# A hybrid attention block on one core: one load queue at the start, and the first norm's row factor moved from the input tiles to the results

## The chip, the core and the metric

The kernel runs on one NeuronCore of a Trainium2 chip. The core has a matrix engine (TensorE, PE in the profile, with its weight loads as PEld), a vector engine (VectorE, DVE), an engine for functions of one operand (ScalarE, ACT), a general one (GpSimd, POOL), and SyncE (SP), which here only issues loads and stores. Matrix products go to PSUM banks; the other tiles lie in SBUF. Loads can be issued from the queues of SP, ACT and POOL. The metric is device time of one execution in microseconds; less is better.

## The reference

One layer of a hybrid block on 256 rows of width 2048, float32. The input is normalised row by row, projected by one wide matrix, mixed by three branches, and followed by a feed-forward part:

```python
def _rms_norm(x, gain):
    xf = x.astype(jnp.float32)
    y = xf * lax.rsqrt(jnp.mean(xf * xf, axis=-1, keepdims=True) + RMS_EPS)
    return (y * gain.astype(jnp.float32)).astype(x.dtype)
...
    u = _rms_norm(x, norm_mix_pre[l])
    mix = hybrid_mixer(u, w_in[l], ...)          # proj = u @ w_in; three branches, gates
    x = x + _rms_norm(mix, norm_mix_post[l])
    hdn = jnp.square(jax.nn.relu(_rms_norm(x, norm_mlp_pre[l]) @ w_mlp_up[l]))
    x = x + _rms_norm(hdn @ w_mlp_down[l], norm_mlp_post[l])
```

The branches are stick-breaking attention and forgetting attention (4 heads of 128 each) and an RWKV-7 time mixing (16 heads of 64). The norm in front of the projection multiplies row t by a factor rstd[t] and column d by a gain. So u @ w = rstd[t] * ((x * gain) @ w): the row factor can be applied to the input tiles or to the result.

## The kernel before

**Tiles and units.** Activations lie transposed, features on partitions and the 256 rows along the free axis, as 16 tiles of 128 features. The precision of float32 is made of two parts: a value is split into a rounded high part and the rest. `split` writes a tile [128, 512] with the high part in columns 0 to 255 and the rest in 256 to 511 (one copy on ACT, one subtraction on DVE). A weight block of 128 x 1024 (512 KB, eight feature tiles by 128 output columns) is loaded into a `raw` buffer and split by `wsplit` into `whi` (ACT, line 152) and `wlo` (DVE, line 153). A half unit is then eight wide products (`whi` with all 512 columns) and eight narrow ones (`wlo` with the high 256 columns); two half units make a unit, 128 output columns in one bank. `evac` empties a bank: it adds the two halves of the columns. `tok` computes value and gate tiles the other way round, with rows on partitions and 512 output columns.

**Order.** `raw`, `whi` and `wlo` have three buffers each. `wnext` keeps one half unit split ahead. Up to the end of the output projection the order on PE is the order of the code (`manual_schedule`, line 247); on the other engines and the queues a planner orders the instructions, and may put one that it holds ready ahead of one written earlier. The mixers (attention, RWKV) run as generators whose steps are placed between the products by an estimated clock (`tick`).

**The start (lines 255 to 354).** The parameters and x (`X0`, 2 MB in four pieces) are issued from ACT's queue, the weights from SP's, in whole blocks of 512 KB. `xsplit` scales x by the gain only and splits it into `xpk`, tiles without the row factor. The first three units (`qb`, weight blocks 0/1, 2/3, 4/5) run interleaved over the first eight tiles and then over the last eight, each product as soon as its tile is there. Five more units on `xpk` follow: together the stick-breaking q and k. After the fourth unit `norm()` squares X0, sums over features by a product with ones, and makes `rstd` as a tile [128, 256] that holds the factor of each row on all partitions. The eight results are multiplied by `rstd` on DVE (line 349). `normed(k)` makes the normalised tiles `upk[k]` from X0, gain and `rstd` (two DVE instructions and one ACT copy each), ten in the loop and six later beside the value tiles. All later units of the projection read `upk`.

**Results.** `shift` (line 520) empties the banks of the RWKV features and mixes each row with the one before; `vtok` (line 908) copies value tiles, `gate` (line 967) takes the tanh of half the gate logits. `rwkv_half` loads a small matrix per pair of heads into the tile `lor` (`lora_load`) and splits it (`lora_split`, line 584).

The loads at the start, as written:

```python
    nc.scalar.dma_start(out=par, in_=params)
    raws = {}
    for a, b, n in ((0, 2, 0), (2, 4, 2), (4, 8, 4), (8, 16, 1)):
        nc.scalar.dma_start(out=X0[:, a:b, :], in_=xt[:, a:b, :])
        raws[n] = wraw(n)
    side.append(lambda: nc.sync.dma_start(out=con, in_=consts[:, 128:]))
    side.append(lambda: nc.sync.dma_start(out=ident, in_=consts[:, 0:128]))
```

## Time and profile before

| | |
|---|---|
| median of 3 runs | 1515.03 us |
| lowest, highest | 1512.64, 1515.22 us |
| the profiled execution's own time | 1514.31 us |
| its span, first to last instruction | 1512.5 us |
| granted TensorE clock, mean | 0.995 |
| moved by DMA | 317.70 MB, mean 210 GB/s |

The profile is one execution. It lists each engine's busy time, the instructions by source line with their mean duration, what ended the idle time before them (the releaser), and the transfers with their time from issue to landing. A matrix product in float32 can show as more than one record. "L153" is line 153 of the kernel. A tile's name stands for all its buffers.

### The profile page before, as it was taken

Reading aid. Unit: us, or ns where it says so; the run is one execution under the profiler, and the core shown is the slowest. Engines: PE = TensorE matmul, PEld = TensorE weight load, DVE = VectorE, ACT = ScalarE, POOL = GpSimd, SP = SyncE. Lnnn points to the kernel's source line nnn. Section 1 sums busy time; section 2 is a strip of 40 time slices with the busy share of each in tenths; the row PEclk is TensorE's granted clock in tenths of the full one; section 3 lists DMA queues with packets and bytes.
Section 4 is the critical chain, followed back from the end, with each engine's and each line's share of the span. In section 5 each row is a group of like instructions: output and inputs, shape, how many; then the busy total and the mean of one; then the engine's idle time right before and its main releaser. Section 6 shows DMA issues by size and latency. Waiting matters only on the chain.

```text
span 1512.5 us, 22758 instructions
## 1 busy us (share of the span) xinstructions
PE 1479.7 (98%) x8387; PEld 1247.3 (82%) x8387; DVE 1213.7 (80%) x1675; ACT 938.4 (62%) x1408; POOL 86.1 (6%) x159
## 2 busy tenths in 40 slices
PE   7999999999999999999999999999999999999997
PEld 6888888887777887788887888888888888888885
DVE  6876677789669799567656788999899999899996
ACT  7665666654566554565444767777677676677662
POOL 0011000100001100000000000000000000000000
PEclk9999999999999999999999999999999999999999
DMA  7555445545544445445784668888879788889884
GB/s 260 184 180 171 164 168 183 172 155 194 182 146 153 166 168 180 160 147 196 252 293 159 219 207 244 245 245 264 265 234 270 243 248 253 254 249 274 251 258 150
DMA packets 107039, 317.70 MB, mean 210 GB/s; under 512 B 10672, under 2 KB 14640, under 8 KB 106544
## 3 DMA queue, kind: packets, MB, share of 16 engines
q1 hardware_dynamic: 93536, 282.76, 54.5%
q0 software_dynamic: 8064, 29.36, 10.4%
q10 hardware_dynamic: 5328, 4.13, 0.8%
q8 instruction: 66, 1.08, 0.3%
q14 instruction: 45, 0.37, 0.1%
HBM read 282.65 MB, written 4.19 MB: 190 GB/s over the span
## 4 chain that ended last, share of the span: by engine, by line
PE 49%; issue 3%; DMA 3%; DVE 1%; ACT 0%; POOL 0%; POOLq 0%; DVEq 0%; ACTq 0%
PE gps L168 13%; PE gps L214 10%; PE gps L172 7%; PE gps L198 3%; PE mps L1324 3%; PE mps L1326 3%; PE mps L1325 3%; PE gps L1326 2%; PE gps L1324 2%; PE gps L1325 2%; PE gps L176 1%; DMA raw<-in_wst_dram 1%; DMA raw<-raw 1%; DMA sp<-raw 1%; DMA sp<-in_wst_dram 1%
## 5 line engine op out<-in xcount | busy, mean ns | idle before, releaser
L153 DVE TENSOR_TENSOR wlo<-raw,whi 128x1024 fp32r<-128x1024 f32 x507 | 616.6, 1225 | 169.4 <-ACT whi L152 155.7
L152 ACT ACTIVATE whi<-raw 128x1024 fp32r<-128x1024 f32 x507 | 532.9, 1056 | 257.1 <-DMA raw<-in_wst_dram 89.8
L168 PE MATMUL gps<-pk,whi 128*128 128x512 f32 x1301 | 330.5, 393 | 0.2 <-DVE pk L1116 0.2
L214 PE MATMUL gps<-whi,pk 128*128 128x512 f32 x1144 | 289.4, 392 | 0.0
L168 PEld LDWEIGHTS gps<-pk,whi 128*128 128x128 f32 x1301 | 241.7, 189 | 47.7 <-DVE pk L1116 0.6
L214 PEld LDWEIGHTS gps<-whi,pk 128*128 128x128 f32 x1144 | 212.7, 188 | 44.2
L172 PEld LDWEIGHTS gps<-pk,wlo 128*128 128x128 f32 x1391 | 189.9, 190 | 13.4 <-DVE wlo L153 0.2
L172 PE MATMUL gps<-pk,wlo 128*128 128x256 f32 x1391 | 195.5, 283 | 0.0
L214 PE MATMUL gps<-wlo,pk 128*128 128x512 f32 x572 | 155.6, 392 | 3.1 <-DVE wlo L153 3.1
L214 PEld LDWEIGHTS gps<-wlo,pk 128*128 128x128 f32 x572 | 106.2, 188 | 26.0 <-DVE wlo L153 3.9
L1190 DVE TENSOR_TENSOR sp<-raw,sp 128x1024 fp32r<-128x1024 f32 x67 | 81.9, 1223 | 6.6 <-ACT sp L1189 6.4
L1189 ACT ACTIVATE sp<-raw 128x1024 fp32r<-128x1024 f32 x67 | 70.5, 1053 | 15.3 <-DMA raw<-in_wst_dram 5.1
L1216 ACT ACTIVATE sp<-gps 128x512 f32<-128x512 f32 x52 | 31.0, 597 | 68.6 <-PE gps L176 68.5
L198 PE MATMUL gps<-whi,pk 128*128 128x512 f32 x264 | 72.3, 396 | 1.1 <-ACT whi L152 1.1
L1324 PE MATMUL mps<-whi,fm 128*128 128x512 f32 x168 | 66.2, 394 | 0.0
L1325 PE MATMUL mps<-whi,fm 128*128 128x512 f32 x168 | 65.9, 392 | 0.0
L1326 PE MATMUL mps<-wlo,fm 128*128 128x512 f32 x168 | 65.6, 391 | 0.0
L198 PEld LDWEIGHTS gps<-whi,pk 128*128 128x128 f32 x264 | 49.6, 190 | 12.2 <-ACT whi L152 1.8
L1286 POOL DMA_DIRECT2D raw<-raw x40 | 34.9, 873 | 428.4 <-DVE raw L1283 132.7
L1326 PE MATMUL gps<-wlo,fm 128*128 128x512 f32 x126 | 49.3, 391 | 0.4 <-DVE wlo L153 0.4
L1324 PE MATMUL gps<-whi,fm 128*128 128x512 f32 x126 | 49.3, 391 | 0.0
L1283 DVE TENSOR_TENSOR raw<-raw,raw 128x1024 f32<-128x1024 f32 x40 | 48.9, 1223 | 0.4
(383 smaller groups left out, 1984.3 us busy)
## 6 DMA issues: line engine op xcount, KB each, us to landing
raw<-in_wst_dram SPq DMA_DIRECT2D x502, 512.0 KB, 4.4
raw<-raw POOLq DMA_DIRECT2D x40, 512.0 KB, 7.5
sp<-in_wst_dram SPq DMA_DIRECT2D x16, 512.0 KB, 6.0
raw<-sp POOLq DMA_DIRECT2D x8, 512.0 KB, 7.3
sp<-raw POOLq DMA_DIRECT2D x8, 512.0 KB, 7.5
x<-in_x_dram SPq DMA_DIRECT2D x8, 256.0 KB, 6.4
xs<-x SPq DMA_DIRECT2D x2, 1024.0 KB, 4.1
x<-xs SPq DMA_DIRECT2D x4, 512.0 KB, 6.0
```

Source lines behind the costliest of these rows:

```text
L152: A.activation(hi, raw, AF.Copy)
L153: V.tensor_tensor(lo, raw, hi.bitcast(F32), ALU.subtract)
L168: PE.matmul(ps, hi[:, i * 128:i * 128 + 128], pks[i], start=first and i == 0, stop=False)
L172: PE.matmul(ps[:, 0:T], lo[:, i * 128:i * 128 + 128], pks[i][:, 0:T], start=False, stop=False)
L198: PE.matmul(ps[tt], pks[k][:, c:c + 128], w[:, (k - k0) * 512:(k - k0) * 512 + 512], start=k == 0 and part == 0 and w is hl[0], stop=w is ...
L214: PE.matmul(ps[tt], pks[k][:, c:c + 128], w[:, (k - k0) * 512:(k - k0) * 512 + 512], start=k == 0 and part == 0 and w is hl[0], stop=False)
L1189: A.activation(hi, raw, AF.Copy)
L1190: V.tensor_tensor(lo, raw, hi.bitcast(F32), ALU.subtract)
L1283: V.tensor_tensor(x, x, z, ALU.add)
L1324: PE.matmul(Q[f], p, w, start=d == 0 and i == 0, stop=False)
L1325: PE.matmul(Q[f], pl, w, start=False, stop=False)
L1326: PE.matmul(Q[f], p, wl, start=False, stop=d == nd - 1 and i == 1)
```

## The change

- All loads of the start are issued from SP's queue in one order, the first weight blocks in halves of 256 KB (512 columns).
- Five products of a zero tile are put on PE ahead of everything.
- The first three units run over tiles 0 to 3, 4 to 7, then 8 to 15, block after block.
- The tiles without row factor take the place of the normalised ones everywhere (`upk`), and `normed` is gone. The factor is applied to results instead: by `scaled` on POOL for q, k and the shifts, and through the scale operand of ACT where `vtok` and `gate` empty banks. For these, rows lie on partitions, so `turned_rstd` turns one row of the mean square into columns by two small products and raises it to the power -0.5 on POOL.
- The squares of the norm are taken earlier, beside the fourth unit's first weight blocks, and pinned in ACT's program order; so are `lora_split`'s copy and one copy in `rwkv_lora`.
- `lor` lies in the buffer of the tile `zx`; `rstd1` has its own.

```diff
+    def pin(ins):
+        return tc.keep_in_program_order(ins)
...
+    zt = rp.tile([128, T], F32, tag="tha", name="zt", bufs=1)
+    V.memset(zt, 0.0)
+    idle = mps()
+    for i in range(5):
+        PE.matmul(idle[:, 0:T], zt[:, 0:128], zt, start=True, stop=True)
+    nc.sync.dma_start(out=par, in_=params)
     raws = {}
-    for a, b, n in ((0, 2, 0), (2, 4, 2), (4, 8, 4), (8, 16, 1)):
-        nc.scalar.dma_start(out=X0[:, a:b, :], in_=xt[:, a:b, :])
-        raws[n] = wraw(n)
+    def load(n, q=None):
+        if n not in raws:
+            raws[n] = wpool.tile([128, HALF], F32, tag="raw", name=nm("raw"), bufs=3)
+        cs = slice(0, HALF) if q is None else slice(512 * q, 512 * q + 512)
+        nc.sync.dma_start(out=raws[n][:, cs], in_=wst[n][:, cs])
+    def loadx(a, b):
+        nc.sync.dma_start(out=X0[:, a:b, :], in_=xt[:, a:b, :])
+    loadx(0, 2)
+    load(0, 0)
+    loadx(2, 4)
+    load(2, 0)
+    load(4, 0)
+    loadx(4, 8)
+    for n in (0, 2, 4):
+        load(n, 1)
+    loadx(8, 12)
...
     def xsplit(k):
...
+        u = pk()
         split(X0[:, k, :], u, P("g1", k))
-        xpk.append(u)
+        upk.append(u)
...
+    def wpart(n, q):
+        if n not in w:
+            w[n] = (wpool.tile([128, HALF], F32R, tag="whi", name=nm("whi"), bufs=3),
+                    wpool.tile([128, HALF], F32R, tag="wlo", name=nm("wlo"), bufs=3))
+        hi, lo = w[n]
+        cs = slice(512 * q, 512 * q + 512)
+        A.activation(hi[:, cs], raws[n][:, cs], AF.Copy)
+        V.tensor_tensor(lo[:, cs], raws[n][:, cs], hi[:, cs].bitcast(F32), ALU.subtract)
+    def prods(n, ks, low):
...
+    for q in range(2):
+        ks = range(4 * q, 4 * q + 4)
+        for k in ks[0:2]:
+            xsplit(k)
+        wpart(0, q)
+        prods(0, ks[0:2], False)
+        for k in ks[2:4]:
+            xsplit(k)
+        prods(0, ks[2:4], False)
+        wpart(2, q)
+        prods(2, ks, False)
+        prods(0, ks, True)
+        wpart(4, q)
+        prods(4, ks, False)
+        prods(2, ks, True)
+        prods(4, ks, True)
+    load(1)
+    loadx(12, 16)
+    for n in (3, 5):
+        load(n)
+    for k in range(8, 12):
+        xsplit(k)
+    for q in range(2):
+        wpart(1, q)
+    prods(1, range(8, 12), False)
+    for k in range(12, 16):
+        xsplit(k)
+    prods(1, range(12, 16), False)
+    prods(1, range(8, 16), True)
+    for n in (3, 5):
+        for q in range(2):
+            wpart(n, q)
+        prods(n, range(8, 16), False)
+        prods(n, range(8, 16), True)
     wpos[0] = 6
-    rstd = rp.tile([128, T], F32, tag="kkr", name="rstd1", bufs=1)
+    rstd = rp.tile([128, T], F32, name="rstd1")
+    rt = cpool.tile([128, 2, 4], F32, name="rt")
+    def squares(i):
+        xf = X0[:, 2 * i:2 * i + 2, :]
+        b = 2 + 2 * (i % 2) if i else 0
+        pin(A.activation(A6[:, b:b + 2, :], xf, AF.Square))
+        if i:
+            V.tensor_tensor(A6[:, 0:2, :], A6[:, 0:2, :], A6[:, b:b + 2, :], ALU.add)
...
-    upk = [pk() for _ in range(KT)]
-    def normed(k):
-        t = tmp()
-        V.scalar_tensor_tensor(t, X0[:, k, :], P("g1", k), rstd, ALU.mult, ALU.mult)
-        split(t, upk[k])
+    def turned_rstd(ms):
+        ps = mps()
+        for tt in range(2):
+            PE.matmul(ps[:, 4 * tt:4 * tt + 4], ms[0:4, tt * 128:tt * 128 + 128], C("ident", slice(0, 4), 0, 4),
+                      start=tt == 0, stop=tt == 1)
+        r8 = rt.rearrange("p a b -> p (a b)")
+        V.tensor_copy(r8, ps[:, 0:8])
+        G.tensor_tensor(r8, r8, cst[:, 2:3].to_broadcast([128, 8]), ALU.pow)
+        V.tensor_scalar(rt[:, :, 1], rt[:, :, 0], 0.5, None, ALU.mult)
+    def scaled(d):
+        G.tensor_tensor(d, d, rstd[0:d.shape[0]], ALU.mult)
+    for i in range(2):
+        wsplit(wraw())
+        if side:
+            side.pop(0)()
+        for k in range(4 * i, 4 * i + 4):
+            squares(k)
     qk = []
     for h in range(8):
-        ps = qb[h] if h < 3 else unit(xpk)
+        ps = qb[h] if h < 3 else unit(upk)
         qk.append(g1())
         evac(ps, qk[h])
         if h == 3:
-            norm()
+            ms = norm()
+        if h == 5:
+            turned_rstd(ms)
         for i in range(h + 1) if h == 3 else [h] if h > 3 else []:
-            V.tensor_tensor(qk[i], qk[i], rstd, ALU.mult)
-        if h >= 3:
-            for k in range(2 * h - 6, 2 * h - 4):
-                normed(k)
-    side.extend(lambda k=k: normed(k) for k in range(10, KT))
+            scaled(qk[i])
...
         V.tensor_tensor(t[0:n], ps[0:n, 0:T], b[0:n], ALU.add)
+        scaled(t[0:n])
...
-        A.activation(z3[96:128], zz[96:128], AF.Copy)
+        pin(A.activation(z3[96:128], zz[96:128], AF.Copy))
...
-                lor[p] = rp.tile([128, 2, 128], F32, tag="lor", name=nm("lor"), bufs=1)
+                lor[p] = rp.tile([128, 2, 128], F32, tag="zx", name=nm("lor"), bufs=1)
...
-                A.activation(wl, raw, AF.Copy)
+                pin(A.activation(wl, raw, AF.Copy))
...
-            A.activation(v, ps, AF.Copy)
+            A.activation(v, ps, AF.Copy, scale=rt[:, len(vs), 0:1])
...
             evac(ps, t)
+            scaled(t)
...
-                A.activation(t, ps[:, i * n:i * n + n], AF.Tanh, scale=0.5)
+                A.activation(t, ps[:, i * n:i * n + n], AF.Tanh, scale=rt[:, len(ths), 1:2])
```

47 lines of the change are left out of this document (9 added, 38 removed).

## The prediction

> **What bounds the kernel now.** I read the page first, then the waits of PE, then its timeline at the start, then busy time by stretches, and last the loads.
>
> ```profile
> span 1512.5 us, 22758 instructions
> PE 1479.7 (98%) x8387; PEld 1247.3 (82%) x8387; DVE 1213.7 (80%) x1675; ACT 938.4 (62%) x1408; POOL 86.1 (6%) x159
> ```
>
> PE is busy for all but 32.8 us, so a change beside PE can only win from those. The waits of PE (line waited for, then total, times and longest in us) say where most of them lie:
>
> ```profile
> PE gps L310 <- ACT whi L152: 8.9, 1, 8.9
> PE gps L214 <- DVE wlo L153: 3.1, 2, 2.0
> PE mps L1100 <- DVE x L1068: 3.0, 1, 3.0
> PE gps L198 <- DVE wlo L153: 2.4, 3, 1.1
> PE gps L310 <- DVE xpk L234: 0.9, 1, 0.9
> ```
>
> The first and last rows, 9.8 us, are L310: the first three units, which the change rewrites. Busy time by stretches (each engine in us, then clock, share of the DMA engines, GB/s) tells where nothing can be won:
>
> ```profile
> 0.00:14.75 14.75, 5.01 (x11) 3.63 (x12) 6.41 (x12) 7.99 (x14) 2.17 (x15) 1.00 0.87 333
> 29.23:330.00 300.77, 300.77 (x1742) 261.93 (x1743) 224.28 (x351) 189.43 (x305) 21.34 (x60) 1.00 0.53 178
> 84.00:313.00 229.00, 229.00 (x1335) 200.71 (x1335) 163.79 (x251) 145.01 (x235) 19.11 (x54) 1.00 0.51 171
> ```
>
> From 29.23 to 330 PE is never idle. So taking work from DVE and ACT there buys nothing, and an earlier start of that stretch moves its end by as much. Only the start counts. PE's timeline there (start, length, line, count):
>
> ```profile
> 8.88 0.80 PE L310 MATMUL gps<-xpk,whi 128*128 128x512 f32 x1 [8.88 <-ACT whi L152]
> ...
> 11.55 1.48 PE L308 MATMUL gps<-xpk,whi 128*128 128x512 f32 x3
> 12.83 1.91 PE L310 MATMUL gps<-xpk,whi 128*128 128x512 f32 x4
> ...
> 18.02 3.04 PE L313 MATMUL gps<-xpk,wlo 128*128 128x256 f32 x24
> 20.89 0.86 PE L310 MATMUL gps<-xpk,whi 128*128 128x512 f32 x3
> ...
> 29.23 2.00 PE L168 MATMUL gps<-xpk,whi 128*128 128x512 f32 x8
> 31.07 1.12 PE L172 MATMUL gps<-xpk,wlo 128*128 128x256 f32 x8
> ```
>
> A wide product costs (31.07 - 29.23) / 8 = 0.23 us, a narrow one (20.89 - 18.02) / 24 = 0.12. One half unit (8 wide, 8 narrow) is 2.8 us, the three first halves are 8.4, and so are the three second halves: 20.89 to 29.23 is 8.34, with no wait. The first halves take 12.0 us from 8.88. Early wide products run at (12.83 - 11.55) / 3 = 0.43 us, half speed.
>
> **The start after the change.** Which loads stand ahead of which decides it. SP's issues, one of its waits, and the landings:
>
> ```profile
> 0.74 1.33 SPq L145 DMA_DIRECT2D raw<-in_wst_dram  x3
> 2.11 0.45 SPq L265 DMA_DIRECT2D con<-in_consts_dram  x1
> 4.64 0.33 SPq L266 DMA_DIRECT2D ident<-in_consts_dram  x1
> 10.11 2.76 SPq L145 DMA_DIRECT2D raw<-in_wst_dram  x2
> ```
> ```profile
> SPq L266 <- DMA raw<-in_wst_dram: 2.1, 1, 2.1
> ```
> ```profile
> raw<-in_wst_dram SPq DMA_DIRECT2D x1, 512.0 KB, 5.6
> ```
> ```profile
> 4.86 0.18 DVE L273 TENSOR_SCALAR omu<-par 128x27 f32<-128x27 f32 x1 [4.86 <-DMA par<-in_params_dram]
> ...
> 7.37 0.51 ACT L233 ACTIVATE xpk<-x,par 128x256 fp32r<-128x256 f32 x1 [4.69 <-DMA x<-in_xt_dram]
> 7.78 1.04 ACT L152 ACTIVATE whi<-raw 128x1024 fp32r<-128x1024 f32 x1
> ```
>
> Two readings. First, the planner issues what is ready: the constants, written behind `raws[1]`, went ahead of it, because its buffer came free only at 10.11. I expect the same after: the queue would run parameters, x and the six half loads, then the last of x and the constants, and only then `load(1)`, which waits for a raw buffer. Second, the fifth issue on SP waited for a landing, so one queue seems to hold four transfers; before, two queues held eight.
>
> *First product.* Ahead of it stand 58 + 256 + 256 KB = 0.58 MB. Before, 333 GB/s x 14.75 us = 4.91 MB came by 14.75, which is just what ends with `raws[1]` (below), and that landed at 15.7: about 1 us from last byte to landing, and 0.39 MB/us if the bytes began near 2.2 us. So 0.58 MB ends near 3.7, and x with half a weight is there between 4.0 and 5.0. Then two splits of x and half a weight copy on ACT (groups of instructions up to 60 us: count, busy us and mean ns of one, idle time before):
>
> ```profile
> L153 DVE TENSOR_TENSOR wlo<-raw,whi 128x1024 fp32r<-128x1024 f32 x18 | 21.8, 1225 | 4.0 <-ACT whi L152 3.3 <-PE gps L313 0.7
> L152 ACT ACTIVATE whi<-raw 128x1024 fp32r<-128x1024 f32 x18 | 18.7, 1053 | 3.2 <-DMA raw<-in_wst_dram 1.9 <-DVE rstd L243 0.8 <-PE gps L310 0.2
> ...
> L233 ACT ACTIVATE xpk<-x,par 128x256 fp32r<-128x256 f32 x13 | 5.8, 498 | 5.6 <-DMA x<-in_xt_dram 5.6
> L234 DVE SCALAR_TENSOR_TENSOR xpk<-x,par,xpk 128x256 fp32r<-128x256 f32 x13 | 5.5, 480 | 2.6 <-ACT xpk L233 2.6
> ...
> L326 DVE TENSOR_TENSOR a<-a 128x512 f32<-128x512 f32 x7 | 4.8, 691 | 0.4
> L338 DVE SCALAR_TENSOR_TENSOR tmp<-x,par,rstd 128x256 f32<-128x256 f32 x9 | 4.2, 488 | 0.0
> L325 ACT ACTIVATE a<-x 128x512 f32<-128x512 f32 x7 | 4.2, 630 | 0.4 <-DVE a L326 0.3
> ...
> L231 DVE TENSOR_TENSOR pk<-tmp,pk 128x256 fp32r<-128x256 f32 x8 | 3.3, 429 | 0.0
> ```
>
> 2 x 0.5 + 0.6 (half of 1.05, with its fixed part) = 1.6: first product at about 5.9 instead of 8.88 (bounds 5.6 and 6.6). The first quarter costs ACT 4 x 0.5 + 3 x 0.6 = 3.8 us and PE 4.2; with x arriving in pieces I add 0.7. First halves end at 5.9 + 0.7 + 8.4 = 15.0.
>
> *Second halves.* Bytes up to and with `load(1)`: parameters 58, x 2048, six halves 1536, constants 576 + 64, `load(1)` 512 KB = 4.91 MB. That is what had come by 14.75 before, and `raws[1]` landed at 10.11 + 5.6 = 15.7. Order within a queue doesn't change that sum. The bounds are 15.7 at the old rate and 17.0 if four transfers in flight carry about a tenth less; I take 16.2. With its first half copied (0.6) PE begins the second halves at 16.8, not 15.0: **the load, not the earlier start, sets it.** 20.89 - 16.8 = 4.1 us won; `load(3)` and `load(5)`, 1.3 us apart, stay ahead of PE's 2.8.
>
> *The five idle products* run while PE has nothing else; with a zero tile they cost the path nothing if they end before 5.9. Ten records at 0.43 are 4.3 us from about 1.3, so 5.6 at the latest. From the rows alone, the slow rate of 0.43 lasted from 8.88 to about 15. The Trainium skill, page "TensorE: Matmul & The Clock Gate", part 1, puts that down to a gate which opens after some 3.4 us of activity seen in a free-running window; the 0.43 agrees with its 427 ns. By it the products may or may not open the gate in time; this is part of rival C.
>
> **What else is added and removed.** Removed: 16 normalisations, on DVE 16 x (0.49 + 0.43) = 14.7 us with a copy each on ACT, and 8 products with rstd on DVE. Worth nothing, since PE was never idle there. The rows for what is added (views of single lines, with min/median/max ns, the groups of POOL, and PE's timeline):
>
> ```profile
> L461 PE MATMUL mps<-ident,foxf x4: 247/248/268, 172.2 to 172.5; 4*128 4x4 f32 x4
> ```
> ```profile
> L661 POOL TENSOR_TENSOR Bt<-kkr,ep 128x256 f32<-128x256 f32 x8 | 6.0, 752 | 2.7 <-DVE kkr L656 2.7
> ```
> ```profile
> L656 DVE SCALAR_TENSOR_TENSOR kkr<-g,par,b x8: 478/838/904, 259.4 to 532.7; 128x256 f32<-128x256 f32 x8
> ```
> ```profile
> L584 ACT ACTIVATE lows<-lor x8: 400/411/419, 30.8 to 515.5; 128x256 fp32r<-128x256 f32 x8
> ```
> ```profile
> 237.25 1.09 PE L607 MATMUL mps<-sqh,bones 128*128 128x512 f32 x4
> ```
>
> - `turned_rstd`: the same form as L461, four records, 0.1 apart: 0.4 us of PE, on the path.
> - 43 factors on POOL (8 q/k, 3 low-rank, 8 fox, 24 shifts) at 0.75: 32 us on an engine that was busy 86 of 1512. Each lengthens the way from bank to result by about 0.9 us. Banks are freed by the addition in front, so PE's next unit doesn't wait. Readers: q and k only behind the value tiles, r, k, v only when the mixers' chain comes to them (PE first needs something made of k at 237.25, L607, though the four k's are the first four of the 24 shifts): covered.
> - POOL against DVE: L656, which begins beside a POOL product, takes up to 0.90 instead of 0.48. 43 x 0.42 = 18 us more on DVE, over units that have 5.6 x (1 - 163.79 / 229) = 1.6 us free each: covered. The Trainium skill, "SBUF — State Buffer", section "SBUF: two separate sides", goes further: the port pair is an exclusive lock for the whole instruction. By it 43 x 0.75 = 32 us; still less than the 65 us that DVE had free there.
> - Pinned copies (L584, eight) can now hold ACT until their small load lands; weights are copied one half unit ahead (2.8 us), which covers a wait of that size.
> - Squares now stand pinned behind the next two weight copies. From `load(1)` at 16.2: raw buffer free 18.2, next weight landed 22.2, copy 1.05, four squares 2.5, copy 1.05, four squares 2.5, last addition 0.7: 30.0. PE reaches the sum at 16.8 + 8.4 + 5.6 = 30.8. Margin 0.8, and ACT is nearly full from 17 to 31 us; I charge 0.3 for this (bounds 0 and 2).
>
> Sum: -4.1 + 0.4 + 0.3 = **-3.4 us**. The profiled execution was 1514.31, 1.8 above its span, so 1510.9 for such a one; the median of the three runs is 0.7 higher, which gives 1511.6. I take the middle, **1511.3**.
>
> **The rivals.**
> - A, the forecast: second halves wait for `load(1)` behind the constants. 1511.3, chance 0.5.
> - B: `load(1)` isn't held (constants behind it, or a quicker queue), PE is the bound: first product 5.9 + 0.7 + 16.8 = 23.4 against 29.23, less 0.4: 5.4 won, 1509.3 (1508.5 if the first product comes at 5.1). Against it stands the order of SP before. 0.16.
> - C: the gain is half lost at once: eight wide and eight narrow products at half speed add 2.4 us (first halves end 17.4 rather than 16.8), one queue carries less (17.0 instead of 16.2), or the sum of squares comes 1 to 2 us late. About -1.5: 1513.2. For it: ACT's fullness and the four in flight. 0.27.
> - D, slower: factors on POOL stretch DVE just where the residues of the weights are due, and PE waits for wlo in the units of the last shifts. Price at most 0.42 a unit; over all 43 that is 18 us, giving 1526 with A's gain. It decides only once a unit's DVE work passes 5.6 us, against 4.0 on average; to end slower by 0.2% it needs 6.5 us lost, in some 16 units. 0.07, near 1518.5.
>
> **How the numbers follow.** 0.2%, 3.0 us, is about what a measurement of this kernel tells from no change: faster means below 1512.0. Faster: most of A (0.44) and B, 0.60. Same: the rest of A and C, 0.33. Slower: D, 0.07. The range takes in B's and C's ends, including the 2 us at the sum: 1508.5 to 1515.0.
>
> **What would show it.** First product at 5.6 to 6.6; constants issued ahead of `load(1)`; PE waiting 1 to 2 us for the copy of that weight near 16; the seventh weight's first product (29.23 before) near 25; no wait of PE from there to 330; the small transposes 0.4 us. It is wrong if PE waits at the sum of squares, if `load(1)` lands before 15, or if the waits behind 330 (L214, L198) change by more than 2 us, since I took that part as unchanged.

## The result, and the profile after

| | before | after |
|---|---|---|
| median | 1513.84 us (4 runs) | 1524.97 us (4 runs, 1521.39 to 1527.22) |
| ratio to before, 95% interval | | 1.0074 (1.0053 to 1.0095) |
| the profiled execution, its span | 1514.31, 1512.5 us | 1527.22, 1525.4 us |

The forecast was 1511.3 us, faster. The kernel became 11 us slower. Below, a ratio is turned into time as (ratio - 1) x 1514: here +11.2 us, between +8.0 and +14.4. Two executions that took far longer (2466 us in e_start_only, 7989 us of the kernel before beside e_unpin_one) are left out of the ratios.

The page of after, its span and its busy times:

```profile
span 1525.4 us, 22769 instructions
...
PE 1489.9 (98%) x8401; PEld 1252.6 (82%) x8401; DVE 1210.7 (79%) x1644; ACT 936.9 (61%) x1398; POOL 137.4 (9%) x203
```

TensorE (PE) still looks full. It was idle for 35.5 us instead of 32.8, but it was also *busy* for 10.2 us longer: 4.6 of them are the idle products of the start, the rest are mostly products that ran slower. VectorE (DVE) has less work than before, GpSimd (POOL) 51 us more. Only the waits and the places tell what happened. The waits of PE in after (line waited for: total us, times, longest us):

```profile
PE mps L696 <- DVE lows L647: 6.9, 2, 4.3
PE gps L214 <- DVE wlo L153: 3.0, 3, 1.7
PE gps L168 <- ACT whi L152: 2.1, 1, 2.1
PE gps L198 <- DVE wlo L153: 2.1, 2, 1.5
...
PE mps L1162 <- DVE x L1130: 1.9, 1, 1.9
PE mps L378 <- DVE a L373: 1.8, 1, 1.8
```

The rows of L214, L198 and L1162 have their like in before (L1162 was L1100). New are L378, the sum of squares; L168, a weight's high part; and L696, the product with the half's small matrix, which waits for DVE's residue (L647).

**Where the time came in.** The same products can be set side by side in PE's two timelines. First after (start, length, line, count, and in brackets the idle time ahead of it):

```profile
1.18 4.63 PE L267 MATMUL mps<-zt 128*128 128x256 f32 x10 [1.18 <-DVE zt L264]
5.70 0.77 PE L328 MATMUL gps<-pk,whi 128*128 128x512 f32 x2
8.48 2.63 PE L328 MATMUL gps<-pk,whi 128*128 128x512 f32 x6 [2.02 <-DVE pk L237]
...
18.23 2.01 PE L328 MATMUL gps<-pk,whi 128*128 128x512 f32 x8
...
26.62 2.00 PE L168 MATMUL gps<-pk,whi 128*128 128x512 f32 x8
...
34.18 1.13 PE L378 MATMUL mps<-a,con 128*128 128x256 f32 x4 [1.81 <-DVE a L373]
...
107.23 2.98 PE L168 MATMUL gps<-pk,whi 128*128 128x512 f32 x8 [2.10 <-ACT whi L152]
110.00 1.84 PE L172 MATMUL gps<-pk,wlo 128*128 128x256 f32 x8
...
262.20 0.98 PE L696 MATMUL mps<-lows 128*128 128x256 f32 x3 [2.62 <-DVE lows L647]
...
488.37 1.13 PE L696 MATMUL mps<-lows 128*128 128x256 f32 x3 [4.29 <-DVE lows L647]
```

And the same places before (L635 is L696):

```profile
104.79 2.00 PE L168 MATMUL gps<-pk,whi 128*128 128x512 f32 x8
...
255.38 0.52 PE L635 MATMUL mps<-lows 128*128 128x256 f32 x3
...
472.34 0.51 PE L635 MATMUL mps<-lows 128*128 128x256 f32 x3
```

Read as a ledger of after minus before: the fourth unit (29.23 in before) comes at 26.62, **-2.6**. At 104.79 / 107.23 it is **+2.4**. At the small matrix's first product, 255.38 / 262.20, it is **+6.8**, at 472.34 / 488.37 **+16.0**, and at the end 1525.4 - 1512.5 = **+12.9**: behind 472 before had stalls of its own that after no longer had. So the start won, and several places behind it lost more. Three of them first, from the trace alone.

**The place at 105 us.** PE waits for ACT's copy of a weight. POOL's timeline in after, then ACT's:

```profile
99.37 2.58 POOL L448 TENSOR_TENSOR sbt<-sbt,con 128x128 f32<-128x128 f32 x2
101.90 0.74 POOL L395 TENSOR_TENSOR g<-g,rstd 128x256 f32<-128x256 f32 x1
102.60 2.48 POOL L448 TENSOR_TENSOR sbt<-sbt,con 128x128 f32<-128x128 f32 x4
```
```profile
105.11 0.84 ACT L454 ACTIVATE sbh<-sbt 128x768 fp32r<-128x768 f32 x1 [2.29 <-POOL sbt L448]
105.86 0.37 ACT L227 ACTIVATE tmp<-gps 128x256 f32<-128x256 f32 x1
106.13 1.99 ACT L152 ACTIVATE whi<-raw 128x1024 fp32r<-128x1024 f32 x2
```

A row factor (L395) stands in POOL's queue among the masks of the attention (L448), ACT's copy of the masked tile waits for the last mask, and the weight copy that PE needs stands behind that copy on ACT. Three queues pass the delay on, none of which is full. Then PE's next sixteen products take 2.98 + 1.84 us instead of the 2.00 + 1.12 that such a group takes (29.23 and 31.07 in the prediction's rows): +1.7 for the slower clock behind a wait of 2.1. The granted clock in stretches of after (between clock and DMA share: each engine's busy time, then clock, share, GB/s):

```profile
103.80:107.20 3.40, 1.33 (x10) 1.01 (x8) 1.75 (x4) 2.08 (x4) 1.28 (x3) 1.00 0.03 11
107.20:110.60 3.40, 3.37 (x11) 2.78 (x12) 3.40 (x5) 2.97 (x5) 1.74 (x2) 0.65 0.33 100
...
262.00:267.00 5.00, 4.80 (x21) 4.26 (x22) 2.17 (x4) 1.57 (x5) 0.00 (x0) 0.68 0.73 237
...
488.30:494.40 6.10, 6.03 (x19) 5.13 (x20) 4.60 (x8) 2.21 (x5) 0.00 (x0) 0.54 0.59 208
```

**The small matrix.** Its copy on ACT is now pinned in program order, so it comes just ahead of its use, where before the planner had taken the first half's forward to 30.8 us (the row of L584 in the prediction) and the second half's, first used at 472.34, to 314.2. ACT's timeline in before:

```profile
314.21 0.41 ACT L584 ACTIVATE lows<-lor 128x256 fp32r<-128x256 f32 x1
```

In after these two copies stand at 257.6 and 481.1. The residue L647 then stands late in DVE's queue. DVE's timeline in after:

```profile
259.10 1.10 DVE L685 TENSOR_TENSOR b<-b 128x512 f32<-128x512 f32 x1
260.13 1.21 DVE L153 TENSOR_TENSOR wlo<-raw,whi 128x1024 fp32r<-128x1024 f32 x1
261.26 0.47 DVE L589 SCALAR_TENSOR_TENSOR g<-tmp,omu,zp 128x256 f32<-128x256 f32 x1
261.77 0.60 DVE L647 TENSOR_TENSOR lows<-lor,lows 64x128 fp32r<-64x128 f32 x2
```

DVE hasn't a gap here. The residue takes 0.6 us and stands behind everything that was put ahead of it; PE has been waiting since 259.58.

**The round trip.** A shift now goes DVE (add, L586), POOL (factor, L395), ACT (scaled copy, L588), DVE (L589): two hops off DVE and back instead of one, and DVE takes its instructions in order. DVE's waits in 47 to 480 us of after:

```profile
DVE wlo L153 <- ACT whi L152: 54.2, 59, 2.9
...
DVE g L589 <- ACT zp L588: 8.7, 8, 1.2
```

In before the idle time that ACT's copy (L527) ended ahead of that step was 0.2 us in 84 to 345 us. Most of this is a wait that moved: in the same stretch DVE waited 16.7 us for ACT's copy of the bank in before (L525), and 9.6 in after (L585), so the two together grew only from 16.9 to 18.3. Whether PE pays for it can't be read off here. The factor alone (its own row: min/median/max ns) took far longer at times than the 0.75 us that I had used:

```profile
L395 POOL TENSOR_TENSOR tmp<-tmp,rstd x27: 726/844/2321, 89.5 to 335.0; 128x256 f32<-128x256 f32 x26, 36x256 f32<-36x256 f32 x1
```

### The profile page after: what moved, and what is told of

Read it like the earlier page. It is cut to its first block, busy times and chain, and to the rows that moved or that the text cites. A ratio compares the mean times of both kernels' runs of the same rounds, so it can differ in the third digit from the quotient of the medians.

```text
span 1525.4 us, 22769 instructions
## 1 busy us (share of the span) xinstructions
PE 1489.9 (98%) x8401; PEld 1252.6 (82%) x8401; DVE 1210.7 (79%) x1644; ACT 936.9 (61%) x1398; POOL 137.4 (9%) x203
## 4 chain that ended last, share of the span: by engine, by line
PE 51%; DVE 2%; DMA 2%; issue 1%; ACT 0%; POOL 0%; POOLq 0%; DVEq 0%; ACTq 0%
PE gps L168 13%; PE gps L214 10%; PE gps L172 7%; PE mps L1386 3%; PE mps L1388 3%; PE mps L1387 3%; PE gps L198 3%; PE gps L1388 2%; PE gps L1386 2%; PE gps L1387 2%; PE gps L176 1%; DVE wlo L153 1%; DMA sp<-raw 1%; DMA sp<-in_wst_dram 1%; DMA raw<-in_wst_dram 1%
## 5 line engine op out<-in xcount | busy, mean ns | idle before, releaser
L153 DVE TENSOR_TENSOR wlo<-raw,whi 128x1024 fp32r<-128x1024 f32 x501 | 613.4, 1232 | 183.2 <-ACT whi L152 171.6
L152 ACT ACTIVATE whi<-raw 128x1024 fp32r<-128x1024 f32 x501 | 526.9, 1056 | 265.6 <-DMA raw<-in_wst_dram 87.0
L168 PE MATMUL gps<-pk,whi 128*128 128x512 f32 x1366 | 347.9, 394 | 2.3 <-ACT whi L152 2.1
L168 PEld LDWEIGHTS gps<-pk,whi 128*128 128x128 f32 x1366 | 253.9, 189 | 52.8 <-ACT whi L152 2.4
L214 PE MATMUL gps<-whi,pk 128*128 128x512 f32 x1144 | 289.4, 392 | 0.0
L214 PEld LDWEIGHTS gps<-whi,pk 128*128 128x128 f32 x1144 | 212.5, 188 | 44.4
L172 PEld LDWEIGHTS gps<-pk,wlo 128*128 128x128 f32 x1456 | 199.6, 191 | 14.4 <-DVE wlo L153 0.2
L172 PE MATMUL gps<-pk,wlo 128*128 128x256 f32 x1456 | 204.7, 283 | 0.0
L214 PE MATMUL gps<-wlo,pk 128*128 128x512 f32 x572 | 156.2, 393 | 3.0 <-DVE wlo L153 3.0
L214 PEld LDWEIGHTS gps<-wlo,pk 128*128 128x128 f32 x572 | 106.3, 188 | 26.5 <-DVE wlo L153 4.6
L198 PE MATMUL gps<-whi,pk 128*128 128x512 f32 x264 | 72.2, 395 | 0.0
L198 PEld LDWEIGHTS gps<-whi,pk 128*128 128x128 f32 x264 | 49.9, 191 | 10.8 <-ACT whi L152 0.2
```

The source lines that it names most:

```text
L152: A.activation(hi, raw, AF.Copy)
L153: V.tensor_tensor(lo, raw, hi.bitcast(F32), ALU.subtract)
L168: PE.matmul(ps, hi[:, i * 128:i * 128 + 128], pks[i], start=first and i == 0, stop=False)
L172: PE.matmul(ps[:, 0:T], lo[:, i * 128:i * 128 + 128], pks[i][:, 0:T], start=False, stop=False)
L198: PE.matmul(ps[tt], pks[k][:, c:c + 128], w[:, (k - k0) * 512:(k - k0) * 512 + 512], start=k == 0 and part == 0 and w is hl[0], stop=w is ...
L214: PE.matmul(ps[tt], pks[k][:, c:c + 128], w[:, (k - k0) * 512:(k - k0) * 512 + 512], start=k == 0 and part == 0 and w is hl[0], stop=False)
```

## The experiments

Two theories at first. **W**: the waits for the small matrix's residue (6.9 us) and what follows them are the loss. **P**: the factors on POOL are the loss, through the round trip. The rest of the names (R, C, S) come in with the expectations. Every ratio is against the kernel before, run beside it on the same chip.

### First four: one part of the change at a time

**e_start_only**: the kernel before with nothing but the new start (queue, idle products, order of the first three units).

> The kernel before with only the new start (one load queue, halves, idle products, new order of the first three units); the normalised tiles and the factor on DVE stay. If the start alone is worth what the changed kernel's first 27 us show (2.6 us) and the norm stands where it did: 1511 to 1512. Rival: the fourth unit's sum of squares is late in this start whatever stands around it, and 2 us are given back: 1513 to 1514.

1510.84 us, ratio 0.9976 (0.9965 to 0.9986): **-3.6 us**, a little under the first range. The lead is kept to the end.

**e_old_start**: the changed kernel with the start of before put back.

> The changed kernel with the start of before (two queues, whole blocks, interleaved units, no idle products); everything on unnormalised tiles as in the change. Theory W: the loss lies behind the start, so it stays: 1524 to 1528. Rival (the start moves the planner's order of everything behind it): 1513 to 1516.

1529.17 us, 1.0099 (1.0078 to 1.0119): +15.0, 1 us above W's range. Both runs agree: the start is worth some 3.6 to 3.8 us wherever it is put, and the rest of the change costs about 15.

**e_scale_dve**: the changed kernel with the factors on DVE.

```diff
-        G.tensor_tensor(d, d, rstd[0:d.shape[0]], ALU.mult)
+        V.tensor_tensor(d, d, rstd[0:d.shape[0]], ALU.mult)
```

> The changed kernel with the 43 factors on DVE instead of POOL. Theory W: the wait near 105 us (2.1 us, with the slow stretch 4.0) goes, the waits at L696 stay in part, since the residue still stands behind the same DVE work: 4 to 6 us less than the changed kernel, 1519 to 1521. Rival P: nearly all of the loss goes, 1513 to 1515.

1517.66 us, 1.0023 (1.0011 to 1.0035): +3.5, 7.7 us of the 11.2 are gone, though DVE now has 43 instructions more. The time lies between the two ranges. The view of that line shows what one costs there, 0.42 us:

```profile
L395 DVE TENSOR_TENSOR tmp<-tmp,rstd x27: 405/425/753, 88.9 to 325.8; 128x256 f32<-128x256 f32 x26, 36x256 f32<-36x256 f32 x1
```

What is left in PE's waits is the small matrix, 5.9 us in two.

**e_lora_early**: the changed kernel with the pinned split of the half's first small matrix put ahead of DVE's correction rounds.

```diff
             A.activation(ri, ri, AF.Exp, scale=-0.5)
+        lora_split(PR[0])
         yield 4.5
...
         At, Bt, Kt, bon = {}, {}, {}, {}
-        lora_split(PR[0])
```

> The changed kernel, with the split of a half's first small matrix written ahead of the two correction rounds on DVE instead of behind them (its copy stays pinned). Theory W (PE waits, each followed by a stretch at half speed): the two waits at L696, 2.6 and 4.3 us, go, and with them the slow stretches behind them; 7 to 9 us less than the changed kernel, about 1517. Rival P (the factors on POOL stretch DVE, so everything is late in many small steps): 0 to 1 us, about 1524.

1524.59 us, 1.0071 (1.0045 to 1.0097): nothing won, though the waits at L696 are gone. PE's largest waits in this kernel:

```profile
PE gps L214 <- DVE wlo L153: 4.5, 5, 1.9
PE gps L198 <- DVE wlo L153: 3.4, 4, 1.4
```

The wait moved on to weight residues. It isn't a clean edit either: DVE stood 3.6 us in front of the residue at its new place, waiting for ACT's copy. So W as the only cause falls; whether the small matrix has a price of its own was still open. By the ledger further down, this kernel loses nothing any more at the two places of the small matrix, but 2.2 us in 258 to 300, 5.7 in 300 to 380 and 1.6 in 380 to 470.

### Second four: order or load

**e_both**: factors on DVE and the split moved, together.

> The changed kernel with both edits of the last runs: the row factors on VectorE, and the split of the half's small matrix put ahead of the correction rounds. What is tested: whether the two delays stand one behind the other (theory S: the small matrix's residue is late only because the round trip TensorE bank - VectorE - GpSimd - ScalarE - VectorE holds VectorE's order, so with the factors on VectorE the moved split costs nothing more) or each has a price of its own. Factors on VectorE alone gave 1517.66 with two waits of the small matrix's product left, 2.0 and 4.3 us (5.9 with the third). Theory S: these 5.9 us go and about 4 of them reach the end: 1512.5 to 1514.5. Rival W2 (VectorE is the bound in 250 to 480 us by its sum of work, whatever the order): the wait moves to the weight residues again, as it did with the split moved alone, and the time is 1516.5 to 1518.5.

1514.16 us, 1.0012 (1.0000 to 1.0024): +1.8. The same move that was worth nothing while the round trip was there is worth 3.5 us of the median (1517.66 to 1514.16) without it, but only 1.7 by the ratios, whose intervals overlap. The time lies in S's range; that the two delays stand one behind the other isn't shown by it.

**e_pool_aside**: the kernel before, with a POOL product of the same size beside each shift and each fox q and k, whose result nobody reads.

```diff
         V.tensor_tensor(t[0:n], ps[0:n, 0:T], b[0:n], ALU.add)
+        pr = rp.tile([128, 4, 128], F32, tag="PB", name=nm("probe"), bufs=1).rearrange("p a b -> p (a b)")
+        G.tensor_tensor(pr[0:n, 0:T], t[0:n], t[0:n], ALU.mult)
         A.activation(zp[0:n, 1:T + 1], t[0:n], AF.Copy, scale=P("mu", i, slice(0, n)))
```

> The kernel before, with one more GpSimd product beside each token shift and each fox q and k (35 in all, about the same places and sizes as the row factors), whose result nobody reads: it adds work, the output is as before. It has the factors' load on GpSimd and on the memory beside VectorE, but is in nobody's order. Theory R (the round trip: VectorE's in-order stream waits for GpSimd's factor through ScalarE's copy) expects no change: 1513 to 1516, with VectorE's weight residues (line 152 of the kernel before) at a mean within 2% of before. Rival C (contention: GpSimd beside VectorE stretches VectorE's instructions) expects longer residues, by 4% and more in 84 to 480 us, and 3 to 8 us more: 1517 to 1523.

1515.23 us, 1.0010 (0.9998 to 1.0023): +1.5, not told from none. POOL's load beside DVE is seen in DVE's rows (here in 84 to 345 us, groups with count, busy us, mean ns):

```profile
L153 DVE TENSOR_TENSOR wlo<-raw,whi 128x1024 fp32r<-128x1024 f32 x82 | 103.3, 1265 | 29.6 <-ACT whi L152 27.1 <-ACT foxt L473 1.0 <-ACT foxt L506 0.8
L530 DVE SCALAR_TENSOR_TENSOR g<-tmp,omu,zp 128x256 f32<-128x256 f32 x24 | 14.1, 587 | 0.3 <-ACT zp L529 0.3
```

In before these groups had means of 1235 and 480 ns: 82 x 0.030 + 24 x 0.107 = 5 us more on DVE, and DVE had the room for it; DVE's busy time on the page, 1218.5 us instead of 1213.7, says the same. The weight residues (L153) are 2.4% longer, between R's 2% and C's 4%; the time is R's. One thing the load alone did reproduce: a wait of 1.6 us for a weight's high part near 105, as POOL's masks stand in the same queue.

**e_sq_free**: the changed kernel with the squares unpinned.

> The changed kernel without the pin that holds ScalarE's squares in program order behind the last weight splits of the start; the planner may then put them where it likes. PE waits 1.8 us for the sum of squares in the changed kernel. If that wait is passed on to the end: the wait goes and the time falls by 1.5 to 2 us (1522.5 to 1523.5). If the delays behind it (small matrix, round trip) hang on VectorE's order and not on where PE stands, the wait goes and nothing is won at the end: 1524 to 1526.

1525.63 us, 1.0086 (1.0071 to 1.0101): the wait of 1.8 us at the sum of squares is gone, and no gain can be measured (the intervals of this run and of after overlap widely); L696 waits 7.6 instead of 6.9.

**e_all3**: factors on DVE, split moved, squares free.

> The changed kernel with all three edits: factors on VectorE, the small matrix's split earlier, the squares unpinned. What is left of the change is then the new start, and the row factor applied behind the banks rather than ahead of the products. The new start alone in the kernel before gave 1510.84. If these three edits name all that costs: 1510 to 1512.5. If working on unnormalised tiles has a further price (43 factors on VectorE at about 0.3 us, 13 us of its time between 47 and 500 us): 1513 to 1516, with waits of PE for weight residues of that sum.

1512.81 us, 0.9996 (0.9986 to 1.0006). It lies 0.3 us above the first expectation's range. Again an edit that was worth nothing alone (the squares) goes with 1.35 us of the median once the delays behind it are away; the intervals of the last two overlap.

### Third four: each suspect alone, in the kernel before

**e_trip_pool** and **e_trip_dve**: a product by one put into the path of 27 shifts and 8 fox q and k, on POOL or on DVE (`X` below).

```diff
         V.tensor_tensor(t[0:n], ps[0:n, 0:T], b[0:n], ALU.add)
+        X.tensor_tensor(t[0:n], t[0:n], cst[0:n, 3:4].to_broadcast([n, T]), ALU.mult)
         A.activation(zp[0:n, 1:T + 1], t[0:n], AF.Copy, scale=P("mu", i, slice(0, n)))
```

> The kernel before, with a GpSimd product by one put into the path of each of its 27 token shifts and of its 8 fox q and k: the output is as before, and nothing else of the change is there (old start, normalised tiles, small matrix as before). The product stands where the row factor stands in the changed kernel, between VectorE's sum and ScalarE's copy, so VectorE's last step of a shift waits for both. Theory R (round trip): between 84 and 480 us VectorE waits in that last step for ScalarE's copy, as in the changed kernel (8.7 us in 84 to 345 us there, 0.2 before), and the time is 1517 to 1523. Rival: the round trip is harmless where the small matrix's split keeps its early place, and the delays of the changed kernel came of the pinned split with it: 1513.5 to 1516, as the product beside the path gave (1515.23).

> The same 35 products by one, in the same places, on VectorE: 35 more instructions of about 0.25 to 0.4 us, 9 to 14 us of VectorE's time, and no change of engine in the path. Theory R: VectorE's order stays whole, and only its sum of work counts where it is the bound: 1514 to 1517. Rival: a step more in the path costs the same on whichever engine: within 2 us of the kernel with the product on GpSimd.

On POOL 1519.59 us, 1.0029 (1.0015 to 1.0044), **+4.4**; on DVE 1513.33, 0.9993 (0.9980 to 1.0005), no change, less than the 1514 to 1517 expected. DVE's wait in its last step of a shift, in the POOL version, 47 to 480 us:

```profile
DVE g L529 <- ACT zp L528: 6.7, 7, 1.1
```

and in the kernel with POOL beside the path it was 0.3 us. So the same 35 instructions cost nothing on the full engine and 4.4 us on the empty one. Path (+4.4) and beside the path (+1.5) overlap in their intervals, and PE's waits don't tell them apart either. First beside the path, then in it:

```profile
PE gps L168 <- ACT whi L152: 1.6, 1, 1.6
```
```profile
PE gps L168 <- ACT whi L152: 1.9, 1, 1.9
```

It is the wait near 105 both times, and only the second has the slower clock behind it (0.51 for 3.5 us; 1.00 beside the path). So these two runs show the price of POOL's queue. That DVE's wait in the last step of a shift costs PE time they don't show.

**e_pin_only**: the kernel before with the copy of the small matrix pinned.

```diff
-                A.activation(wl, raw, AF.Copy)
+                tc.keep_in_program_order(A.activation(wl, raw, AF.Copy))
```

> The kernel before, with ScalarE's copy of the half's small matrix held in program order as the changed kernel holds it; nothing else is changed. In the kernel before the planner had taken it forward to the first 40 us. If the pinned place alone makes TensorE wait for the residue (6.9 us in three waits in the changed kernel): waits of TensorE for the small matrix's residue of 2 to 7 us and 1516 to 1521. If it takes the round trip ahead of it to make the residue late: no such wait over 0.5 us and 1513 to 1515.

1517.43 us, 1.0028 (1.0014 to 1.0043), **+4.2**. The wait is there without any round trip:

```profile
PE mps L635 <- DVE lows L586: 4.0, 2, 3.4
```

**e_probe**: the kernel before with two added waits of PE, each for a chain of POOL products made from fox k (1 product at k 0, 4 at k 3); the products are unused.

> The kernel before, with two added waits of TensorE and nothing else: a small product (4 columns, its result unused) that reads a GpSimd scratch tile made from fox k 0 by one GpSimd product, and from fox k 3 by four in a row. It prices a stall of TensorE by itself. If a stall costs its own length: the time grows by the two waits of the trace, about 1 and 3 to 4 us, 1517 to 1519. If TensorE runs at half its clock for a stretch behind a stall: half-speed stretches of about 3.4 us behind one or both in the trace and up to 1.7 us more for each, 1519 to 1522. If a stall is taken back by idle time of TensorE later: less than the sum of the waits.

1524.90 us, 1.0070 (1.0042 to 1.0098): +10.6 for 6.5 us of waits, above all three ranges, since the waits were longer than I had thought. Waits, and the clock in stretches:

```profile
PE mps L953 <- POOL probe L952: 6.5, 2, 4.9
```
```profile
118.00:124.00 6.00, 5.93 (x34) 5.25 (x35) 3.53 (x5) 1.07 (x2) 0.32 (x2) 1.00 0.30 98
137.80:142.70 4.90, 0.05 (x1) 0.00 (x0) 1.68 (x2) 1.33 (x2) 3.64 (x4) 0.78 0.39 154
142.74:149.50 6.76, 6.76 (x23) 5.69 (x24) 0.85 (x2) 1.67 (x3) 0.53 (x1) 0.66 0.02 7
```

Behind the wait of 1.6 us (ending at 118.1) the clock stayed full, behind the one of 4.9 (ending at 142.7) it fell to 0.66 for 6.8 us, which is 6.8 x 0.34 = 2.3 us of full-speed work lost. A stall of PE costs its length and sometimes a second part behind it, and here none of it was taken back up to 495 us: against before, PE's products are 9.3 us late at 250 and still 9.3 at 495.

### Last: do the parts add up

**e_trip_pin**: both suspects together in the kernel before.

> The kernel before with both parts together: the GpSimd product by one in the path of the 27 token shifts and 8 fox q and k, and the pinned split of the small matrix; old start, normalised tiles; the output is as before. Alone they gave +5.3 and +3.1. Sum: 1522 to 1523.5. If they multiply: 1525 to 1530, near the changed kernel with the old start (1529.17), with two or three waits for the residue of 6 us and more together.

**e_lora_unpin**: the changed kernel with that one pin taken away.

> The changed kernel without the pin on ScalarE's copy of the half's small matrix; the row factors stay on GpSimd. The planner then takes the first copy and its residue forward again, out of the stretch behind 245 us. The parts so far, each alone in the kernel before: new start -3.2 us (1510.84 beside 1514), GpSimd in the path +5.3, pinned split +3.1. If the changed kernel is the sum of independent parts, taking the pin away gives 3 us back: 1521 to 1523. If the pinned split and the round trip multiply (both stand in one order of VectorE, and the residue is late by what VectorE waited for the round trip): 6 us or more come back, 1515.5 to 1519, no wait of TensorE for the residue over 0.5 us, and the VectorE waits for ScalarE's copy (8.7 us) stay.

1522.35 us, 1.0068 (1.0048 to 1.0088), +10.3, and 1521.37, 1.0053 (1.0036 to 1.0069), +8.0; the second median is 3.6 us below that of after. Both are the sum by their medians, as the first expectation of each has it. By their totals the parts don't multiply.

**e_start_trip**: the new start and the product by one on POOL, in the kernel before.

> The kernel before with the new start and the GpSimd product by one in the 35 paths; normalised tiles, small matrix as before, output as before. Alone the start gave -3.2 us (1510.84) and the product +5.3 (1519.59, beside 1514.3). If these two add: 1515 to 1517.5, and the 4 to 5 us that the changed kernel without its pin has above that (1521.37, 1520.37 with the product by one) belong to the unnormalised tiles: eight more factors ahead of 100 us and the order that follows from them. If the start's gain is lost once VectorE is late (TensorE comes earlier to residues that come no earlier): 1519 to 1521.5, the same as the product alone, with a lead of 2 us at 29 us that is gone by 380 us.

1516.27 us, 1.0020 (1.0006 to 1.0035), +3.0: in their totals, gain and loss add as well.

**e_unpin_one**: e_lora_unpin with the factor's tile replaced by a column of ones. **e_free_pool**: e_lora_unpin with the squares free too.

> The changed kernel with the split unpinned (1521.37), whose 43 GpSimd factors now multiply by one column read over and over instead of by the tile of row factors: the row normalisation of the first half is left out, nothing else. It prices the factor's second full operand. In the stretch behind 300 us the factors took 1250 ns in the mean and VectorE waited 3.5 us for ScalarE's copies behind them; the product by one column in the kernel before took 867 ns there, VectorE waited 1.0 us and TensorE not at all. Theory R2 (what is left, some 5 us, is the length of the real factor beside VectorE, through the round trip): means under 1000 ns, waits of VectorE for the copies as in the kernel with the product by one (6.7 us in all or fewer), and the time falls by 3 to 5 us: 1516.5 to 1518.5. Rival: the rest is the unnormalised tiles' other work (eight more factors ahead of 100 us, the order that the planner gives them): it stays at 1520 to 1522.

> The changed kernel without both pins (small matrix, squares), the row factors on GpSimd as the change has them. New start and product by one together gave 1516.27; the changed kernel without the pin of the small matrix 1521.37, and in its ledger of product starts 2.2 of these 5 us are there by 45 us: TensorE's wait for the sum of squares and the products that turn the row factors. If these reach the end now that the small matrix is out of the way: 1519 to 1520, the wait of 1.9 us for the sum of squares gone. If VectorE behind 250 us takes them back, as it did where the squares alone were freed (1525.63): 1521 to 1522.

1520.37 us, 1.0046 (1.0032 to 1.0059), and 1520.30, 1.0039 (1.0022 to 1.0057). By the medians each is about 1 us below e_lora_unpin, by the ratios 1.1 and 2.1, and the intervals overlap: neither forecast of a clear gain is borne out. The first lies in its rival's range, the second between its two.

**e_free_dve**: the changed kernel with factors on DVE and without the pins of the squares and of the small matrix: all that was found, taken out. The pin of the one copy in `rwkv_lora` stays; it was never tried alone.

> The changed kernel with the factors on VectorE and without the two pins (squares, small matrix): the change with all that was found taken out. The changed kernel with factors on VectorE, the split moved earlier by hand and the squares free gave 1512.81; the start alone in the kernel before 1510.84. If the unnormalised tiles are worth anything by themselves: under 1510. If they are worth nothing, since TensorE never waited for the normalised tiles, and cost 43 VectorE instructions: 1511 to 1513.

1511.87 us, 0.9983 (0.9973 to 0.9993), -2.6, beside -3.6 (-5.3 to -2.1) for the start alone. The intervals overlap: the unnormalised tiles are worth nothing that these runs can measure, on either side.

| in the kernel before | us from the ratio (interval) |
|---|---|
| new start | -3.6 (-5.3 to -2.1) |
| POOL product in 35 paths | +4.4 (+2.3 to +6.7) |
| pinned split | +4.2 (+2.1 to +6.5) |
| sum of the three | +5.0 |
| the change | +11.2 (+8.0 to +14.4) |

The change is 6 us above that sum. The same two steps show it twice: e_lora_unpin (+8.0) lies 5 above e_start_trip (+3.0), and e_old_start (+15.0) 5 above e_trip_pin (+10.3).

### Where each kernel loses: the ledger by stretches

To place the parts, I took from each trace the starts of the same PE products as in before and their differences, at eleven times of before; a number below is what a stretch adds to the difference (us; one profiled execution each, so that half a us is nothing). For the change the seven sum to +14.3; what lies between and behind them is -1.4, which makes the 12.9 above. That execution is the slowest of its four. Behind 495 us, where the kernels no longer differ, the profiles drift apart by up to 4 us (e_free_dve -3.9, e_trip_pool +3.1), so a row of the table doesn't add up to a run's time.

| kernel | to 29 | 29-47 | 102-125 | 250-258 | 300-380 | 470-479 | 479-495 |
|---|---|---|---|---|---|---|---|
| the change | -2.6 | +2.8 | +3.8 | +4.3 | +4.2 | +4.9 | -3.1 |
| e_old_start | +0.4 | +2.6 | +2.3 | +5.0 | +3.9 | +4.1 | -3.1 |
| e_sq_free | -2.2 | +0.7 | +3.9 | +3.6 | +4.2 | +4.8 | -3.0 |
| e_lora_unpin | -2.7 | +2.9 | +3.8 | 0.0 | +5.5 | +0.1 | -1.6 |
| e_free_pool | -2.5 | +0.7 | +2.3 | 0.0 | +5.2 | 0.0 | 0.0 |
| e_unpin_one | -1.4 | +2.9 | +2.1 | 0.0 | +3.3 | 0.0 | -1.6 |
| e_scale_dve | -3.3 | +2.9 | +0.2 | +1.9 | +0.8 | +4.2 | -3.1 |
| e_free_dve | -2.7 | +0.8 | +0.2 | 0.0 | +0.5 | +0.1 | -1.6 |
| e_start_only | -2.1 | 0.0 | 0.0 | 0.0 | +0.5 | 0.0 | -1.5 |
| e_start_trip | -2.1 | 0.0 | +2.2 | 0.0 | +3.4 | 0.0 | -1.5 |
| e_trip_pool | -0.4 | 0.0 | +3.8 | 0.0 | +0.4 | 0.0 | -1.6 |
| e_trip_pin | -0.2 | 0.0 | +2.1 | +4.0 | +2.9 | +4.1 | -3.1 |
| e_pin_only | -0.6 | 0.0 | 0.0 | +1.0 | -0.1 | +4.4 | -3.1 |
| e_pool_aside | +0.8 | 0.0 | +1.8 | 0.0 | +0.4 | 0.0 | -1.6 |
| e_trip_dve | +0.1 | 0.0 | 0.0 | 0.0 | +0.4 | 0.0 | 0.0 |

Read down the columns, each has one owner:

- **29-47**, the sum of squares and the turned factors: 2.6 to 2.9 with the pinned squares, 0.7 to 0.8 with free ones, 0 in the kernels that normalise as before.
- **102-125**, POOL's queue: 1.8 to 3.9 wherever POOL has the 35 or 43 products, in the path or beside it, and at most 0.2 where it has not. It is a wait of 1.6 to 2.1 us. The four kernels at 3.8 and 3.9 have the slow clock behind it, the others have not.
- **250-258 and 470-479**, the pin: 0 at both in every kernel without it. At the second it is 4.1 to 4.9 whatever else is changed. At the first it is 1.0 alone, 1.9 with the factors on DVE and 3.6 to 5.0 with POOL in the path. Here two parts make each other worse.
- **300-380**, the round trip: 2.9 to 5.5 wherever POOL stands in the path, except in e_trip_pool (0.4); 0.9 or less where the product is on DVE, beside the path or absent. Here too the parts don't add: e_trip_pool has 0.4 and e_pin_only -0.1, but e_trip_pin 2.9. POOL is shown as the cause by e_free_pool (5.2) against e_free_dve (0.5) and by e_start_trip (3.4) against e_start_only (0.5). That it is the order and not POOL's load beside DVE is not shown: beside the path was tried only in the kernel before, where the path loses nothing either.
- **479-495**: before itself has two waits of 1.15 and 1.13 us and a stretch of slow clock there that the others don't all have; the kernels get back 0 to 3.1 there, most of it where they had lost it just ahead, at the pin.

So the 5 us that seemed left over (e_lora_unpin against e_start_trip; 6.3 between the two profiles) are the sum of squares (2.9 against 0.0), 2 us more of the round trip (5.5 against 3.4) and the slow clock behind the wait near 105 (3.8 against 2.2), less 0.6 at the start. That the product by a column costs less there (3.3 in e_unpin_one) goes with the factor's second full operand, but 1 us between two medians doesn't show it. **Open** stays why e_trip_pool goes free in 300-380 while the same product with the new start loses 3.4: DVE waited for ACT's copies 7.4 us in 240 to 380 us there, in e_trip_pool 3.1, and what makes the difference wasn't tried. It isn't the new start alone, since e_trip_pin has the old one. Open too is why the 2.1 us that free squares win in the second column (e_sq_free) are not in that kernel's time: its profile is still 2.2 us ahead of after's at 495 us and loses that behind it, and the intervals of the two don't exclude a gain of 2 us.

The fastest of all these by its median is **e_start_only**, 0.24% below the kernel before and 14 us below the changed one; e_free_dve can't be told from it.

## Why the prediction was wrong

- **Bound: half right.** That PE's removed neighbours are worth nothing was right: e_free_dve does without the sixteen normalisations and gains no more than the start. The step that followed from it, that nothing behind 29 us changes, was wrong. "PE is never idle from 29.23 to 330" says that all deliveries came in time; it doesn't say by how much. I took the room from busy time (DVE 65 us free in 84 to 313), but the room that counts is that of the single delivery: at 107, 262 and 488 us one came 2.1 to 4.3 us too late. The waits that I had named as a sign of being wrong, L214 and L198, hardly changed (5.1 us of waits for residues against 5.5); the loss came at others.
- **The start: right in size, not in its reason.** First product 5.70 (forecast 5.9). Then PE waited 2.02 us for the second pair of x tiles, first halves ended at 18.2 rather than 15.0, and PE, not `load(1)`, set the second halves: 18.23 instead of 16.8. Won at the fourth unit: 29.23 - 26.62 = 2.6 of the 4.1, and 3.6 at the end where the start is alone (in its profile 2.1 of it stand at 29 us and 1.5 come in 479 to 495, where before has a slow stretch that this execution lacks). The constants were not issued ahead of `load(1)`, and the queue took more than four transfers. It was rival C's course: the first halves at half speed behind the wait of 2.02 (clock 0.65 at 8 to 12 us) and the sum of squares late. SP's issues of after show the order, with the eleventh issue at 6.03 and the constants at 18.31, and `load(1)` waiting for its buffer until 12.13:

```profile
6.03 0.68 SPq L279 DMA_DIRECT2D x<-in_xt_dram  x1
12.13 0.33 SPq L276 DMA_DIRECT2D raw<-in_wst_dram  x1
...
18.31 0.43 SPq L290 DMA_DIRECT2D con<-in_consts_dram  x1
```

- **Squares: margin 0.8, charged 0.3, measured 1.8.** That PE waits there was a sign of being wrong that I had named. The wait is inside the bounds (0 to 2) that I gave; with the turned products it is the 2.8 of the ledger's second column, where I had 0.7.
- **"43 factors on POOL ... covered": the step that failed first.** It counted readers, found none in a hurry, and put the term at nothing. It didn't count what stands in *order* with the factor: POOL's queue holds the masks (3.8 us at 105, wait and slow clock together), and DVE's last step of a shift holds DVE until the factor and ACT's copy are done. In 300 to 380 the factors on POOL cost 4.2 us; that this is by DVE's order is argued from DVE's waits (7.4 us in e_start_trip, 3.1 in e_trip_pool, which loses nothing there), not shown.
- **"Pinned copies ... covers a wait of that size": the second.** I asked whether ACT would be held by the load. What the pin did was to take away the planner's early place of the copy, and so the residue came at the end of DVE's queue: 4.0 us of waits and +4.2 alone (e_pin_only), 4.3 and 4.9 in the change's ledger, of which up to 3.1 came back in 479 to 495.
- **POOL against DVE.** Estimated 18 us of DVE time, and 32 by the rule of the Trainium skill, "SBUF — State Buffer", section "SBUF: two separate sides". Measured 5 with 35 products (e_pool_aside), and I had rightly said that this is covered. The trace shows some stretching, as the rule has it, but far less than if every product had shut DVE out for its whole length; how often the two met at all wasn't counted.
- **Rival D** had the right side, slower, and in part the right place (residues of the weights late in the shifts, in 300 to 380), and a chance of 0.07. It counted on stretching; the places at 105 and at the small matrix were waits in order, for which the sum of work that I tested it against (5.6 us a unit) is no measure. Its 1526 also takes A's gain off twice: 1511.3 + 18 is 1529.3.
- **What a wait costs.** Half speed stood in the forecast for the start alone (rival C); in after it also follows the waits at 107, 262 and 488.

## What to carry to other kernels

Moving an operation from a full engine to an empty one adds two hand-overs to the path, and engines take their instructions in order: look at what stands behind the two waiting instructions, and at what else is in the empty engine's queue. A busy share shows room for work, not room for lateness; to tell them apart, run the same operation once beside the path and once in it, in the very kernel that loses the time. Differences of 2 us between single profiles can be the slow clock behind one wait, which the same wait has in one kernel and not in another. Where a matmul engine is never idle, list for each stretch how late a delivery may be before calling a delay covered; and before an instruction is pinned, see where the planner had it.

## What the runs showed of the hardware

- Behind waits of PE of 2.1, 2.6 and 4.3 us in after, and 4.9 in e_probe, the granted clock was 0.54 to 0.68 for some 3 to 7 us; behind 1.6 it stayed 1.00. The Trainium skill, "TensorE: Matmul & The Clock Gate", "HAM oscillation — how this bites in real kernels", gives the rule as no idle gaps over about 3.4 us. Here the clock fell behind two gaps well under that. It isn't every such gap: behind the wait near 105 it fell in after, e_sq_free, e_lora_unpin and e_trip_pool (waits of 1.9 to 2.1 us, 3.8 or 3.9 in the ledger's third column) and stayed full in the others (1.6 to 2.1 us of wait, 1.8 to 2.3 in the ledger). In before, two waits of 1.15 and 1.13 us, ending at 480.5 and 482.8, were enough (0.73 in 480 to 486); in e_start_only the same two, 1.12 and 1.11, were not (1.00). What decides it no run here shows.
- A POOL product of two float32 tiles [128, 256] took 726 to 2321 ns (after), on DVE 405 to 753 (e_scale_dve).
- The new start, with eleven issues from one queue in 6 us, moved less at first than the old one with two queues: at 4 to 8 us 285 GB/s (320 in e_start_only) against 380 in before, at 8 to 12 us 369 (387) against 418. The pieces and their order differ too, so that the one queue is the cause isn't shown. Stretches of after (the last two figures are the DMA share and GB/s):

```profile
4.00:8.00 4.00, 2.46 (x7) 1.25 (x5) 1.64 (x4) 2.03 (x5) 0.00 (x0) 1.00 0.81 285
8.00:12.00 4.00, 3.52 (x11) 2.88 (x12) 3.59 (x7) 3.40 (x8) 0.00 (x0) 0.65 0.94 369
```
